# Tiles of both ends of SBUF moved to multiples of 512 bytes in a one-core S5, convolution and FFN trunk

## The chip, the core and the metric

The kernel runs on one core of a Trainium2 chip. The metric is device time in microseconds: 2323.66 us before (median of 3 runs, 2323.28 to 2326.3). The engines are named as in the profile: PE (TensorE, the matmuls), PEld (its weight loads), DVE (VectorE), ACT (ScalarE), POOL (GpSimd) and SP (SyncE, which here only starts transfers).

## The reference: what is computed

A two-layer trunk over 1024 positions of width 1024, all float32. Layer 0 mixes tokens with an S5 state-space mixer and a GLU, layer 1 with a gated width-3 convolution. Each is followed by a SwiGLU FFN (hidden 2816) and a gated per-layer input; a last RMSNorm ends it.

```python
for i in range(DEPTH):                       # DEPTH = 2
    hn = rmsnorm(h, norm_mix_g[i])
    mix = s5_mixer(hn, ...) if i % 2 == 0 else shortconv_mixer(hn, ...)
    h = h + mix
    h = h + swiglu_ffn(rmsnorm(h, norm_ffn_g[i]), ffn_w_in[i], ffn_w_out[i])
    gate = sigmoid(rmsnorm(h, norm_ple_g[i]) @ ple_w_gate[i])
    h = h + gate * (p[i] @ ple_w_up[i])
return rmsnorm(h, final_norm_g)
# s5_mixer: 64 groups of 64 complex states and 16 channels; gelu(y) @ w_glu; val * sigmoid(gate)
```

## The kernel before

**Split products.** Each float32 matrix is split into a high and a low part in the type float32r, and a product is three matmuls (`mm3`, lines 122 to 124): high by high, high by low, low by high. The first operand of `PE.matmul` after the output is the stationary one, which a weight load brings into the array (128 columns, 512 bytes per partition); the second moves through it (512 columns, 2048 bytes). In the profile's rows the moving operand is named first: `psmm<-uhigh,ws` has `uhigh` moving and `ws` stationary.

**Stages.** First the S5 stage: constants, then eight blocks of eight groups, with the two up-projections `p @ ple_w_up` (`pstu`, written out by `up<-ev`) as filler. Then GLU, FFN 0 in, FFN 0 out, the gated input of layer 0 (PLE), convolution in and out, FFN 1 in and out, PLE 1 and the final norm. The input stages (FFN in, convolution in) use `block_product`, a Strassen-like scheme of seven products of four 128-row slices with three matmuls each, 84 in all; products 0 to 3 stream `ulow`, 4 to 6 stream `uhigh`, and the weights `ws` are stationary. In the output stages the hidden tile `ch` is stationary and the weight units stream; units lie in `ulow`, `uhigh` or the four tiles `w8`. In GLU and PLE the activations in `ulow` are stationary and units in `uhigh` or `w8` stream.

**Memory.** Pools grow from both ends of SBUF. From the left: the constants (`ident`, `mhalf`, `identn`, `sgnA`, `sgnN`, `r8`, `rstd`, `cw`), then `ulow` (64 KB), then `h` and whatever the stage needs: `ws`, `st`, `hs`, `w8`, `t2` tiles. From the right: `rawp` (the four slots `raw` and `ch` and, in part, `xn`), and below it first the S5 constants (pool `s5g`, named `gen`: tables `ptab`, their scratch `ph`, `wbt`, `kp`, `dd`), later `uhigh` (48 KB). All big tiles are whole multiples of 512 bytes, so their starts modulo 512 are set by what lies at the two ends:

| tile | start before | modulo 512 | start after | modulo 512 |
|---|---|---|---|---|
| ulow | 18016 | 96 | 17408 | 0 |
| ws (lowest) | 83552 | 96 | 82944 | 0 |
| w8 (lowest, highest) | 116320, 140896 | 96 | 115712, 140288 | 0 |
| uhigh | 163808 | 480 | 163328 | 0 |
| ch, raw (lowest, highest) | 212960, 225248 | 480 | 212480, 224768 | 0 |
| t2 tiles (512 columns) | from 153440 | 352 | from 152832 | 256 |
| M, U, E, W2, tmp (S5, left) | from 120416 | 96 | from 120320 | 0 |

All slices that matmuls take of these tiles begin at multiples of 512 bytes within the tile, except in the S5 stage's own tiles.

**Order.** The order on each engine is made by a list scheduler with a simulated timeline when the kernel is built; there is no written order. It honours dependencies between tiles that share a buffer: a tile under an old tag waits until the old tile's last reader is done. DMAs are started by SP in order, the E swaps, spills and hidden stores by POOL in order.

**An S5 block b.** `gen_in` makes U and wbt, `gen_out` makes W1 and the kernel taps `kp` (16 rows), `dd` is the skip connection's diagonal, added to `kp` on POOL (line 937); `gen_toeplitz` spreads `kp` into M by eight DMAs on SP (line 950). `states` (line 963) makes pb; `scan` multiplies pb by the phases E into `tmp`, swaps its halves by two DMAs (`tw<-tmp`, line 698), adds (`sv`), scans on DVE (line 982) into `gv`, and `outputs` (lines 997 to 999) multiplies M, W1 and W2. The phase table of two blocks, `ptab`, is built on DVE by doubling in `phases`, with the scratch tile `ph`; `gen_phase` swaps it into E by four DMAs on POOL (line 957).

Of the kernel before, what the change touches and what calls it, by code (L numbers as in the profile page):

```python
# [9 lines left out]
F32 = mybir.dt.float32  # L10
F32R = mybir.dt.float32r
# [6 lines left out]

P = 128
MAGIC = 12582912.0  # L20


@with_exitstack
def trunk(
# [8 lines left out]
    V, A, G, PE = nc.vector, nc.scalar, nc.gpsimd, nc.tensor  # L33
# [8 lines left out]
    NG, NP = s5_a_re.shape[1], s5_a_re.shape[2]  # L42
    KG = D // NG
# [4 lines left out]
    const = ctx.enter_context(tc.tile_pool(name="const", bufs=1))  # L48
# [6 lines left out]
    ident = const.tile([P, P], F32, name="ident")  # L55
    make_identity(nc, ident)
    mhalf = const.tile([P, T], F32, name="mhalf")
    V.memset(mhalf, -0.5)
    identn = const.tile([P, P], F32R, name="identn")
    A.mul(identn, ident, -1.0)  # L60

# [13 lines left out]
    evp = tc.alloc_tile_pool(name="evp", bufs=2)  # L77
# [4 lines left out]
    def psum(pool=None):  # L82
        pool = pool or mm
        return pool.tile([P, 512], F32, name="ps" + pool.name, tag="ps")
# [521 lines left out]
    GB = P // KG  # L606
# [4 lines left out]
    for tl, v in ((sgnA, 1.0), (sgnN, -1.0)):  # L611
        V.memset(tl[R0], v)
        V.memset(tl[R1], -v)
    r8 = const.tile([P, NG], F32, name="r8")
    rstd = const.tile([P, T], F32, name="rstd")

    rawp = ctx.enter_context(tc.tile_pool(name="rawp", bufs=1, side="right"))
    gen = tc.alloc_tile_pool(name="s5g", bufs=1, side="right")
    st = tc.alloc_tile_pool(name="s5t", bufs=1, side="right")

    def small(shape=(P, NG), dt=F32):
        return st.tile(list(shape), dt, name="sm", tag="sm", bufs=28)

    def ts(o, a, s1, op0, s2=None, op1=None):
        if op1 is None:
            V.tensor_scalar(o, a, s1, None, op0)
        else:
            V.tensor_scalar(o, a, s1, s2, op0, op1)
        return o

    def tt(o, a, b, op):
        V.tensor_tensor(o, a, b, op)  # L632
        return o

    def stt(o, a, s, b, op0, op1):
        V.scalar_tensor_tensor(o, a, s, b, op0, op1)
        return o

    def exp_to(o, a, shape):
        n = small(shape)  # L640
        ts(n, a, 1.4426950408889634, ALU.mult, MAGIC, ALU.add)
        ts(n, n, -MAGIC, ALU.add, 129.0, ALU.min)
        ts(n, n, -127.0, ALU.max)
# [86 lines left out]
    kq = small()  # L730
    ts(kq, ang, 2.0 / math.pi, ALU.mult, MAGIC, ALU.add)
    ts(kq, kq, -MAGIC, ALU.add)
    r = small()
# [3 lines left out]
    m4 = small()  # L737
    ts(m4, kq, 0.25, ALU.mult, MAGIC, ALU.add)
    ts(m4, m4, -MAGIC, ALU.add)
    stt(m4, m4, -4.0, kq, ALU.mult, ALU.add)  # L740
# [114 lines left out]
    NJ = P // 2  # L855
    LB = 2
    LQ = LB * HQ
# [6 lines left out]
    def tmp_tile():  # L864
        return run.tile([P, GB * P], F32, name="tmp", tag="tmp", bufs=2)
# [50 lines left out]
    def gen_out(b):  # L916

        gsl = slice(b * GB, (b + 1) * GB)
        shp = [P, GB, NL, KG]
        W1 = Ws[b] = run.tile(shp, F32, name="W1", tag="W1", bufs=2)  # L920
        A.copy(W1[:, :, 0, :], cA[:, gsl])
        shp1 = [P, GB, T, KG]
        tm = tmp_tile()[:, 0:GB * P].rearrange("p (g s k) -> p g s k", g=GB, s=T)
        for o, pw, cc in ((W1[:, :, 1:NL, :], pwr, cA), (tm, pwn, cS)):
            tt(o, pw[:, gsl, 1:NL].unsqueeze(3).broadcast_to(shp1), cc[:, gsl].unsqueeze(2).broadcast_to(shp1), ALU.mult)
        tt(W1[:, :, 1:NL, :], W1[:, :, 1:NL, :], tm, ALU.subtract)
        kp = kps[b] = gen.tile([KG, GB, T, KG], F32, name="kp", tag="kp")
        for hf in range(2):
            pk = psum(tr)
            for c in range(4):  # L930
                PE.matmul(pk[0:KG, c * P:(c + 1) * P], bbA[:, b * GB + 4 * hf + c, :], W1[:, 4 * hf + c, 0:T, :],  # L931
                          start=True, stop=True)
            A.copy(kp[:, 4 * hf:4 * hf + 4].rearrange("p g s k -> p (g s k)"), pk[0:KG, :])
        dd = gen.tile([KG, GB, KG], F32, name="dd", tag="dd")
        G.tensor_tensor(dd, ident[:KG, :KG].unsqueeze(1).broadcast_to([KG, GB, KG]),
                        dk[:, gsl].unsqueeze(2).broadcast_to([KG, GB, KG]), ALU.mult)
        G.tensor_tensor(kp[:, :, 0, :], kp[:, :, 0, :], dd, ALU.add)
# [75 lines left out]
    states(0)  # L1013
    gen_phase(0)
    gen_out(0)
    gen_swap(0)
    gen_toeplitz(0, M)
    gen_in(1)
    for b in range(NBT):
        scan(b)  # L1020
        nx = b + 1
        if nx < NBT - 1:
            if b % LB == 0 and b // LB + 1 < NBT // LB:
                phases(b // LB + 1)
            gen_out(nx)
            zt = outputs(b)
            gen_phase(nx)
            states(nx)
            gen_swap(nx)
            gen_toeplitz(nx, M)  # L1030
            if b + 2 < NBT:
                gen_in(b + 2)
            channels(b, zt)
        elif nx < NBT:
            states(nx)
            gen_phase(nx)
            gen_out(nx)
            M = run.tile([P, GB, P], F32, name="M", tag="E", bufs=2)
            G.memset(M, 0.0)
            gen_toeplitz(nx, M)  # L1040
            zt = outputs(b)
            channels(b, zt)
            gen_swap(nx)
        else:
            zt = outputs(b)
# [118 lines left out]
```

## Time and profile before

| | |
|---|---|
| median of 3 runs | 2323.66 us |
| the profiled execution | 2323.06 us, of which the span is 2321.3 us |
| mean granted TensorE clock | 0.987 |
| PE, DVE, ACT, POOL busy | 96%, 57%, 33%, 7% |
| transfers waited for in the chain that ended last | DMA 3% |

The page lists groups of equal instructions by line, engine and operands: count, busy time, mean ns of one, idle time of the engine before them and what ended it. Matmuls overlap, and the end of each is modelled, so the distance from one start to the next is what tells their pace. The timeline gives a start, a duration and a merged count per row. A stretch of the view by windows gives each engine's busy time with the number of instructions.

### The profile page before, as it was taken

The page shows a single profiled execution, that of the slowest core. Times are in us where ns is not written, and L with a number is a line of the kernel's source. Part 1 is how long each engine was busy: PE and PEld are TensorE (multiplying, and loading weights), DVE is VectorE, ACT ScalarE, POOL GpSimd, SP SyncE. Part 2 cuts the span into 40 slices and gives each one's busy share as a digit, 9 for nine tenths or more (in the row PEclk, how much of TensorE's full clock was granted, in tenths as well). Part 3 has the DMA queues.
Part 4 walks back from the last instruction along what each step waited for, and adds up shares of the span by engine and source line. Part 5 has one row for each costly group of instructions (what it writes and reads, how often), then busy time and mean ns, then how long its engine had stood idle before and what let it go on. Part 6 is the DMA issues. An engine that isn't in the chain of part 4 may idle for free.

```text
span 2321.3 us, 27094 instructions
## 1 busy us (share of the span) xinstructions
PE 2240.0 (96%) x10253; PEld 1832.0 (79%) x10253; DVE 1331.0 (57%) x2244; ACT 765.3 (33%) x1449; POOL 161.8 (7%) x268
## 2 busy tenths in 40 slices
PE   6987999899999999999989999979999999999998
PEld 5776887688888888888868888868888888888887
DVE  7885325866666642224488776486666666222444
ACT  6554223433333320013343332253333333100232
POOL 2110001000000000000010000010000000000000
PEclk9999999999999999999989999989999999999999
DMA  7656201333333365433232234544333334643323
GB/s 245 149 138 150 70 19 69 103 109 109 109 109 109 109 227 181 149 119 114 89 111 84 92 94 152 192 131 118 109 109 109 109 109 141 231 163 123 127 87 109
DMA packets 212978, 288.87 MB, mean 124 GB/s; under 512 B 21360, under 2 KB 152432, under 8 KB 212848
## 3 DMA queue, kind: packets, MB, share of 16 engines
q1 hardware_dynamic: 191520, 212.63, 29.3%
q0 software_dynamic: 20928, 74.47, 10.4%
q8 instruction: 80, 1.31, 0.2%
q14 instruction: 50, 0.41, 0.1%
q10 hardware_dynamic: 400, 0.04, 0.0%
HBM read 190.93 MB, written 79.69 MB: 117 GB/s over the span
## 4 chain that ended last, share of the span: by engine, by line
PE 91%; DVE 4%; DMA 3%; ACT 1%; SPq 1%; issue 1%; POOL 0%; DVEq 0%; POOLq 0%; ACTq 0%
PE psmm L122 29%; PE psmm L124 29%; PE psmm L123 29%; PE pstr L185 1%; PE pstr L997 1%; DVE W L632 1%; DMA raw<-in_ffn_w_in_dram 1%; PE pstr L998 0%; PE pstr L999 0%; PE pstr L931 0%; DMA tw<-tmp 0%; DVE gv L982 0%; DVE tmp L632 0%; DVE xn L177 0%; PE pstu L122 0%
## 5 line engine op out<-in xcount | busy, mean ns | idle before, releaser
L122 PE MATMUL psmm<-ulow,ws 128*128 128x512 f32 x896 | 351.8, 394 | 5.7 <-ACT ws L87 3.1
L123 PE MATMUL psmm<-ulow,ws 128*128 128x512 f32 x896 | 351.5, 393 | 2.5 <-DVE ulow L88 2.5
L124 PE MATMUL psmm<-ulow,ws 128*128 128x512 f32 x896 | 351.4, 393 | 2.0 <-DVE ws L88 2.0
L124 PE MATMUL psmm<-uhigh,ws 128*128 128x512 f32 x672 | 265.3, 395 | 0.0
L122 PE MATMUL psmm<-uhigh,ws 128*128 128x512 f32 x672 | 265.0, 395 | 0.0
L123 PE MATMUL psmm<-uhigh,ws 128*128 128x512 f32 x672 | 264.9, 394 | 0.0
L409 DVE TENSOR_TENSOR h<-psmm,h 128x512 f32<-128x512 f32 x128 | 88.3, 690 | 234.4 <-PE psmm L124 234.4
L88 DVE TENSOR_TENSOR ws<-raw,ws 128x512 fp32r<-128x512 f32 x224 | 153.6, 688 | 115.1 <-ACT ws L87 115.0
L87 ACT CAST ws<-raw 128x512 fp32r<-128x512 f32 x224 | 137.8, 619 | 208.7 <-PE psmm L124 201.9
L122 PEld LDWEIGHTS psmm<-ulow,ws 128*128 128x128 f32 x896 | 169.6, 189 | 43.6 <-ACT ws L87 4.2
L123 PEld LDWEIGHTS psmm<-ulow,ws 128*128 128x128 f32 x896 | 169.6, 189 | 39.7 <-DVE ulow L88 3.5
L124 PEld LDWEIGHTS psmm<-ulow,ws 128*128 128x128 f32 x896 | 169.5, 189 | 39.1 <-DVE ws L88 3.0
L123 PE MATMUL psmm<-ulow,ch 128*128 128x512 f32 x448 | 177.2, 396 | 0.0
L122 PE MATMUL psmm<-ulow,ch 128*128 128x512 f32 x448 | 176.9, 395 | 0.0
L124 PE MATMUL psmm<-ulow,ch 128*128 128x512 f32 x448 | 176.9, 395 | 0.0
L87 ACT CAST ws<-st 128x512 fp32r<-128x512 f32 x168 | 104.2, 620 | 211.9 <-PE psmm L124 192.1
L123 PEld LDWEIGHTS psmm<-uhigh,ws 128*128 128x128 f32 x672 | 126.2, 188 | 30.3
L124 PEld LDWEIGHTS psmm<-uhigh,ws 128*128 128x128 f32 x672 | 126.1, 188 | 30.3
L122 PEld LDWEIGHTS psmm<-uhigh,ws 128*128 128x128 f32 x672 | 126.2, 188 | 29.0
L370 POOL DMA_DIRECT2D hid<-hs x104 | 78.1, 754 | 917.6 <-DVE hs L88 908.7
L140 ACT ACTIVATE junk<-h 128x512 bf16<-128x512 f32 (+1 forms) x113 | 64.1, 567 | 207.6 <-DVE h L409 122.8
L88 DVE TENSOR_TENSOR ws<-st,ws 128x512 fp32r<-128x512 f32 x168 | 115.2, 686 | 1.3 <-ACT ws L87 1.2
(241 smaller groups left out, 3997.9 us busy)
## 6 DMA issues: line engine op xcount, KB each, us to landing
hid<-hs POOLq DMA_DIRECT2D x104, 512.0 KB, 4.3
ch<-hid SPq DMA_DIRECT2D x96, 512.0 KB, 3.8
raw<-in_ffn_w_in_dram SPq DMA_DIRECT2D x88, 512.0 KB, 4.4
raw<-in_ffn_w_out_dram SPq DMA_DIRECT2D x44, 512.0 KB, 4.0
hd<-h POOLq DMA_DIRECT2D x24, 512.0 KB, 2.9
h<-hd SPq DMA_DIRECT2D x24, 512.0 KB, 5.8
raw<-in_conv_w_in_dram SPq DMA_DIRECT2D x24, 512.0 KB, 3.9
up<-ev SPq DMA_DIRECT2D x32, 256.0 KB, 3.2
```

Source lines behind the costliest of these rows:

```text
L87: A.copy(hi, src)
L88: V.tensor_tensor(lo, src, hi.bitcast(F32), ALU.subtract)
L122: PE.matmul(ps, ahi, bhi, start=start, stop=False, skip_group_check=more)
L123: PE.matmul(ps, ahi, blo, start=False, stop=False, skip_group_check=more)
L124: PE.matmul(ps, alo, bhi, start=False, stop=stop, skip_group_check=more)
L140: done["square"] = A.activation(junk[:, cs], h[t][:, cs], AF.Square, scale=1.0 / math.sqrt(D), accum_out=ms).ins
L185: PE.transpose(pt[:, c * P:(c + 1) * P], xn[:, kt * P:(kt + 1) * P], ident)
L370: nc.gpsimd.dma_start(out=hid[ht // 4][half * HT:(half + 1) * HT, :, ht % 4].rearrange("t p l j -> p t l j"), in_=hs.bitcast(F32))
L409: done["sum"] = V.tensor_tensor(h[t][:, cs], ps[nb], h[t][:, cs], ALU.add).ins
L632: V.tensor_tensor(o, a, b, op)
L997: PE.matmul(o, Us[b][:, g, :], Ms[b][:, g, :], start=True, stop=False)
```

## The change

`identn`, `r8` and `dd` leave their places: `identn` goes into the pool of evacuation tiles (left, above `h`), `r8` into `gen`, and `dd` takes part of the scratch tile `ph`. A constant `lead` of 160 bytes is added at the left, and a tile `edge` of 480 bytes, which nothing reads or writes, at the right end. The starts that follow are in the table above. `ident` stays 128 bytes over a multiple of 512.

```diff
+EDGE = 120
@@
-    identn = const.tile([P, P], F32R, name="identn")
-    A.mul(identn, ident, -1.0)
+    lead = const.tile([P, 40], F32, name="lead")
@@
-    r8 = const.tile([P, NG], F32, name="r8")
     rstd = const.tile([P, T], F32, name="rstd")
 
+    edge = ctx.enter_context(tc.tile_pool(name="edge", bufs=1, side="right"))
+    edge.tile([P, EDGE], F32, name="edge")
     rawp = ctx.enter_context(tc.tile_pool(name="rawp", bufs=1, side="right"))
     gen = tc.alloc_tile_pool(name="s5g", bufs=1, side="right")
+    r8 = gen.tile([P, NG], F32, name="r8")
+    identn = evp.tile([P, P], F32R, name="identn", bufs=1)
+    A.mul(identn, ident, -1.0)
@@
-        dd = gen.tile([KG, GB, KG], F32, name="dd", tag="dd")
+        dd = gen.tile([P, LQ * NJ], F32, name="dd", tag="ph")[0:KG, 0:P].rearrange("p (g k) -> p g k", g=GB)
         G.tensor_tensor(dd, ident[:KG, :KG].unsqueeze(1).broadcast_to([KG, GB, KG]),
                         dk[:, gsl].unsqueeze(2).broadcast_to([KG, GB, KG]), ALU.mult)
         G.tensor_tensor(kp[:, :, 0, :], kp[:, :, 0, :], dd, ALU.add)
```

The instructions are the same in number and kind. The scheduler puts some in another order, most of all in the S5 stage. On POOL, from block 0 to block 2 (`kp_1081` and `kp_1086` belong to block 1, `E_1294` and `E_1299` to block 2), before:

```order
L957 DMA E_1126<-ptab_886 64x2x256 x4
L984 MEMSET tmp_1036 128x8
L937 TENSOR_TENSOR kp_939<-kp_939,dd_952 16x8x16
L935 TENSOR_TENSOR dd_1094<-ident_72,dk_438 16x128
L937 TENSOR_TENSOR kp_1081<-kp_1081,dd_1094 16x8x16
L935 TENSOR_TENSOR dd_1262<-ident_72,dk_438 16x128
L984 MEMSET tmp_1237 128x8
L957 DMA E_1294<-ptab_1042 64x2x256 x4
L957 DMA E_1495<-ptab_1042 64x2x256 x4
L937 TENSOR_TENSOR kp_1249<-kp_1249,dd_1262 16x8x16
```

and after (lines are 4 higher there):

```order
L961 DMA E_1131<-ptab_891 64x2x256 x4
L988 MEMSET tmp_1041 128x8
L941 TENSOR_TENSOR kp_944<-kp_944,dd_957 16x8x16
L988 MEMSET tmp_1242 128x8
L939 TENSOR_TENSOR dd_1099<-ident_72,dk_443 16x128
L961 DMA E_1299<-ptab_1047 64x2x256 x4
L941 TENSOR_TENSOR kp_1086<-kp_1086,dd_1099 16x8x16
L939 TENSOR_TENSOR dd_1267<-ident_72,dk_443 16x128
L961 DMA E_1500<-ptab_1047 64x2x256 x4
L941 TENSOR_TENSOR kp_1254<-kp_1254,dd_1267 16x8x16
```

The add into block 1's `kp` stood ahead of the E swaps of block 2, which read the new table; now it stands behind them, and its `dd` waits for the table's last step. Blocks 3 and 5 are moved in the same way.

On DVE, the scan of block 3 with the end of the table for blocks 4 and 5 (`tmp` is what the tw swap sends, `sv<-sv,tw` what waits for it), before:

```order
L636 SCALAR_TENSOR_TENSOR tmp<-pb,sgnA,E 128x8x63
L632 TENSOR_TENSOR ptab<-ptab,ph 128x8x8 x2
L636 SCALAR_TENSOR_TENSOR tmp<-pb,sgnN,E 128x8x64
L632 TENSOR_TENSOR sv<-pb,E 128x8x63
L632 TENSOR_TENSOR sv<-pb,E 128x8x64
L632 TENSOR_TENSOR ph<-ptab,ew 128x256
L632 TENSOR_TENSOR ptab<-ptab,ew 128x16x16
L632 TENSOR_TENSOR ptab<-ptab,ph 128x8x16 x2
L632 TENSOR_TENSOR ph<-ptab,ew 128x512
L632 TENSOR_TENSOR ptab<-ptab,ew 128x16x32
L632 TENSOR_TENSOR sv<-sv,tw 128x8x127
L632 TENSOR_TENSOR ptab<-ptab,ph 128x8x32 x2
```

and after:

```order
L636 TENSOR_TENSOR ph<-ptab,ew 128x256
L636 TENSOR_TENSOR ptab<-ptab,ew 128x16x16
L636 TENSOR_TENSOR ptab<-ptab,ph 128x8x16 x2
L640 SCALAR_TENSOR_TENSOR tmp<-pb,sgnA,E 128x8x63
L636 TENSOR_TENSOR ph<-ptab,ew 128x512
L636 TENSOR_TENSOR ptab<-ptab,ew 128x16x32
L640 SCALAR_TENSOR_TENSOR tmp<-pb,sgnN,E 128x8x64
L636 TENSOR_TENSOR sv<-pb,E 128x8x63
L636 TENSOR_TENSOR sv<-pb,E 128x8x64
L636 TENSOR_TENSOR ptab<-ptab,ph 128x8x32 x2
L636 TENSOR_TENSOR sv<-sv,tw 128x8x127
```

The table's last two doublings, all but their final pair, stand ahead of `tmp` now, and the final pair ahead of `sv<-sv,tw`. In the GLU and all later stages the order of the products is the same up to a few places among neighbouring instructions.

## The prediction

> **What bounds the kernel now.** I read the page first: busy time, then the chain that ended last.
>
> ```profile
> span 2321.3 us, 27094 instructions
> PE 2240.0 (96%) x10253; PEld 1832.0 (79%) x10253; DVE 1331.0 (57%) x2244; ACT 765.3 (33%) x1449; POOL 161.8 (7%) x268
> PE 91%; DVE 4%; DMA 3%; ACT 1%; SPq 1%; issue 1%; POOL 0%; DVEq 0%; POOLq 0%; ACTq 0%
> ```
>
> TensorE is busy for 96% of the span and makes up 91% of the chain. That is a mean over stages, so next comes the view of busy time by stretch, one stretch for each kind of stage. Its columns are PE, PEld, DVE, ACT, POOL, granted clock, DMA share, GB/s.
>
> ```profile
> 240.00:360.00 120.00, 120.00 (x522) 97.83 (x522) 29.71 (x71) 26.68 (x77) 0.00 (x0) 1.00 0.08 26
> 480.00:820.00 340.00, 340.00 (x1482) 277.95 (x1481) 222.22 (x349) 121.65 (x211) 26.95 (x36) 1.00 0.38 112
> 1250.00:1440.00 190.00, 190.00 (x829) 155.25 (x828) 138.50 (x204) 62.04 (x95) 13.16 (x25) 1.00 0.33 106
> 0.00:220.00 220.00, 178.53 (x1171) 149.92 (x1171) 167.64 (x429) 121.82 (x291) 36.33 (x71) 0.95 0.65 169
> ```
>
> In the GLU (240 to 360 us), the first FFN (480 to 820) and the convolution's input products (1250 to 1440) TensorE never pauses, at granted clock 1.00, and the next busiest engine, VectorE, has 27% of its time left even in the tightest (138.50 of 190). There only the step from one matmul to the next sets the time. The S5 stage (0 to 220) is different: TensorE 178.53 of 220 us, VectorE 167.64, DMA share 0.65; they wait for one another in turn.
>
> So the question is what a matmul's step depends on. The timeline of TensorE answers it, if one takes the first and last row of stretches in which one kind of matmul runs without a break. The operand named first streams ("moving"), the second is loaded as weights ("stationary"); `w` is the tile w8.
>
> ```profile
> 266.54 0.39 PE L122 MATMUL psmm<-w,ulow 128*128 128x512 f32 x1
> ...
> 309.86 0.39 PE L124 MATMUL psmm<-w,ulow 128*128 128x512 f32 x1
> 310.08 0.40 PE L122 MATMUL psmm<-uhigh,ulow 128*128 128x512 f32 x1
> ...
> 354.65 0.39 PE L124 MATMUL psmm<-uhigh,ulow 128*128 128x512 f32 x1
> 499.44 0.39 PE L123 MATMUL psmm<-ulow,ws 128*128 128x512 f32 x1
> ...
> 507.17 0.39 PE L124 MATMUL psmm<-ulow,ws 128*128 128x512 f32 x1
> 507.39 0.40 PE L122 MATMUL psmm<-uhigh,ws 128*128 128x512 f32 x1
> ...
> 512.75 0.39 PE L124 MATMUL psmm<-uhigh,ws 128*128 128x512 f32 x1
> 843.77 0.40 PE L122 MATMUL psmm<-ulow,ch 128*128 128x512 f32 x1
> ...
> 933.14 0.39 PE L124 MATMUL psmm<-ulow,ch 128*128 128x512 f32 x1
> 933.37 0.39 PE L122 MATMUL psmm<-uhigh,ch 128*128 128x512 f32 x1
> ...
> 944.34 0.39 PE L122 MATMUL psmm<-uhigh,ch 128*128 128x512 f32 x1
> ```
>
> The duration column (0.39 or 0.40) is modelled and tells nothing; the steps do. `w,ulow`: 192 matmuls (8 row tiles of 8 x 3), 43.32 us over 191 steps, 226.8 ns. `uhigh,ulow`: 192, 44.57 us over 191, 233.4 ns. `ulow,ws`: 35 in 7.73 us, 227.4 ns. `uhigh,ws`: 24 in 5.36 us, 233.0 ns. `ulow,ch`: 384 (8 row tiles, 2 halves, 8 hidden tiles x 3), 89.37 us over 383 steps, 233.3 ns. From 933.37 to 944.34 stand one row tile's 48 matmuls, 36 `uhigh,ch` and 12 `w,ch`; with the 12 at 233.3, the 36 take (10.97 - 2.80)/36 = 226.9 ns.
>
> Neither operand explains this alone: `ulow` moves at 227.4 with `ws` and at 233.3 with `ch`; `uhigh` moves at 233.0 with `ws` and at 226.9 with `ch`. The pair does. `ulow`, `ws` and `w8` are tiles of the left end (96 over a multiple of 512 bytes), `uhigh` and `ch` of the right end (480 over). **Both operands from one end: 227.0 ns. One from each end: 233.2 ns.** The two left starts in `w,ulow` are up to 120 KB apart and the step is still the short one, so distance as such is not it. Within one end all slices differ by multiples of 512 bytes; across the ends the difference is 384 over such a multiple.
>
> **The change, part by part.** First, all large tiles of both ends now start at multiples of 512 bytes, so every pair stands as pairs within one end do today. How many matmuls have one operand from each end is in the groups by line; L123 and L124 have equal counts, so each row stands for three.
>
> ```profile
> L122 PE MATMUL psmm<-uhigh,ws 128*128 128x512 f32 x672 | 265.0, 395 | 0.0
> L122 PE MATMUL psmm<-ulow,ch 128*128 128x512 f32 x448 | 176.9, 395 | 0.0
> L122 PE MATMUL psmm<-uhigh,ulow 128*128 128x512 f32 x256 | 100.9, 397 | 0.6 <-ACT uhigh L87 0.6
> L122 PE MATMUL psmm<-w,ch 128*128 128x512 f32 x192 | 76.2, 397 | 0.0
> L122 PE MATMUL psmm<-ulow,ws 128*128 128x512 f32 x896 | 351.8, 394 | 5.7 <-ACT ws L87 3.1 <-ACT ulow L87 1.9 <-ACT s L348 0.7
> L122 PE MATMUL psmm<-w,ulow 128*128 128x512 f32 x248 | 96.9, 391 | 0.0
> L122 PE MATMUL psmm<-uhigh,ch 128*128 128x512 f32 x192 | 74.8, 390 | 0.0
> ```
>
> Mixed pairs: 3 x (672 + 448 + 256 + 192) = 4704. One-end pairs: 3 x (896 + 248 + 192) = 4008. At 233.2 - 227.0 = 6.2 ns, little of it behind waits (idle before the mixed groups is 0.0 to 0.6 us), the first term is 4704 x 6.2 ns = **-29 us**. Bounds: 0, if the ends and not the offsets matter; and -29 - 111 = -140, if landing on a 512 multiple also removes what a one-end pair still pays (third rival). I take -29, since both offsets that the trace shows (96 with 96, 480 with 480) give the same 227 ns: the difference between the two counts, not the offset itself.
>
> A rule of the Trainium skill speaks against this term. "SBUF — State Buffer" (Who interferes with whom) gives TensorE two read ports, one for the moving operand and one for the weight load, and calls them independent. By that rule the weights' place could not matter to the step and the term would be 0 (the first rival); the 233.3 beside 226.9 ns for the same `ch` disagrees with it.
>
> Second, the diagonal term `dd` now lives in the phase table's scratch tile `ph`, and the scheduler has moved work in the S5 stage. GpSimd must wait to write `dd` until VectorE has finished the current table, and four E swaps now stand between `dd` and the add into `kp`. `kp` feeds the eight M transfers on SP, and M the outputs' first matmul (L997). Rows of the timeline for block 1 (73.84 to 95.76) and block 3 (120.11 to 137.98), and the landing row of tile M:
>
> ```profile
> 73.84 1.02 POOL L937 TENSOR_TENSOR kp<-kp,dd 16x128 f32<-16x128 f32 x1 [14.96 <-DMA up<-ev]
> 87.94 0.73 DVE L632 TENSOR_TENSOR ptab<-ptab,ph 128x256 f32<-128x256 f32 x2
> 88.97 2.41 POOL L957 DMA_DIRECT2D E<-ptab  x4 [8.42 <-DVE ptab L632]
> 85.80 3.84 SPq L950 DMA_DIRECT2D M<-kp  x6
> 95.76 0.49 PE L997 MATMUL pstr<-M,U 128*128 128x128 f32 x2
> 120.11 0.41 DVE L632 TENSOR_TENSOR ph<-ptab,ew 128x256 f32<-128x256 f32 x1
> ...
> 122.03 0.68 DVE L632 TENSOR_TENSOR ptab<-ptab,ew 128x512 f32<-128x512 f32 x1
> 124.71 0.75 DVE L632 TENSOR_TENSOR ptab<-ptab,ph 128x256 f32<-128x256 f32 x2
> 137.98 0.49 PE L997 MATMUL pstr<-M,U 128*128 128x128 f32 x2
> DMA to landing us min/median/max: 1.9/2.7/7.1
> ```
>
> Block 1: the table ends at 88.67; `dd` (0.4, estimated from the add's kind), four E swaps 2.41 and an add of at most 1.02 bring `kp` to 92 instead of 74.9; eight M issues at 0.64 (3.84/6) end at 97, and 1.9 to 2.7 to land makes 99 to 99.8 against an L997 at 95.76: 3 to 4 us late. Queued behind L997 on TensorE are the other output products and the next block's transposes, behind M on SP the tw transfers of block 2. Half of it, +2, I let reach the end, since VectorE waits for tw there anyway. Block 3: the table ends at 125.46 and L997 stands at 137.98; 0.4 + 2.41 + 1.02 + 5.1 + 2.7 = 11.6 us still fit between. But five table steps, 2.6 us (120.11 to 122.71), now stand ahead of the `tmp` that releases tw, where before they filled the wait for tw; in exchange the last pair (0.75) moves ahead of `sv`: +1.9. Block 5 has two such steps of the 0.41 kind: +0.8. Together +4.7, and as a few short steps also move into block 2's wait, I take **+4 us**, with bounds -2 (the trade only swaps idle time) and +8 (all of 4 + 2.6 + 0.8 reaches the end).
>
> Third, `identn` (into the evacuation pool) and `r8` (into the S5 pool) are the same instructions at other addresses. VectorE's and ScalarE's operands already come from both ends: priced 0. DMA: VectorE waits for tw for 23.7 us in the S5 stage, eight times; were aligned rows 10% quicker, 2 us would go, so 0 with a bound of -2.
>
> ```profile
> DVE sv L632 <- DMA tw<-tmp: 23.7, 8, 5.5
> ```
>
> The profiled execution took 2323.06 us (span 2321.3 and 1.8 around it), 0.6 under the median of the runs. 2323.1 - 29 + 4 = 2298, as a median 2298.7.
>
> **The rivals.** *The ends decide, not the offsets* (13%): something between the two regions, such as memory split into parts, lengthens mixed pairs wherever they start. `uhigh` begins some 15 KB above the highest `w8`, and a border there would look the same in this trace; against it, operands in separate parts should disturb each other less. Then only S5 moves: 2323.1 + 4 + 0.6 = 2328.
>
> *Half of it* (8%): the mixed steps alternate or keep part of their price, say 3 ns: -15 + 4, 2313.
>
> *Multiples of 512 remove more* (5%). What a one-end pair pays beyond streaming can be read where the last tile's matmuls are 256 wide:
>
> ```profile
> 2307.76 0.28 PE L122 MATMUL psmm<-w,ulow 128*128 128x256 f32 x1
> ...
> 2309.44 0.28 PE L124 MATMUL psmm<-w,ulow 128*128 128x256 f32 x1
> ```
>
> 14 steps in 1.68 us, 120.0 ns, against 226.8 for 512: 0.417 ns a column, so 12.8 ns a matmul are fixed. If that is a cost of starting 32 bytes off and goes, 8712 x 12.8 = 111 us more: 2187. Against it: 96 and 480 pay alike. "TensorE: Matmul & The Clock Gate" of the Trainium skill (Wait — 56ns, not 53.3ns?) has 215.7 ns back to back at 512 columns, which would be 11 ns under the trace's best; no run here shows it.
>
> *Slower: equal offsets collide* (5%). At a multiple of 512 both streams of every pair open the same line or bank, and the 6.2 ns falls on the 4008 one-end pairs too, while the mixed keep theirs: +25 + 4, 2352. It decides from the first GLU matmul on (266 us). Against it, equal offsets are today's quick case.
>
> **How the numbers follow.** Alike offsets 69%, own range 2291 to 2304 (S5 -2 to +8, step 5.7 to 6.5 ns). Range 2290 to 2328: it takes in the half case and the first rival. A change under 0.2% (4.6 us) is about what a measurement of this kernel cannot tell from none. Faster: 69 + 8 + 5 and a lucky 1 of the first rival, 83%. The first rival's 2328 lies just within 0.2%: 8% same, and 4% with the 5% of the collision slower, 9%.
>
> **What would show it.** Right: `uhigh,ws`, `ulow,ch`, `uhigh,ulow` and `w,ch` step at 227 like `ulow,ws`; a row tile of `uhigh,ch` and `w,ch` takes 10.90 us, not 10.97; FFN tiles come every 84 x 227 = 19.07 us, not 19.29; GLU starts 2 to 8 us later than 221.7 and everything after it has gained 29. Wrong: mixed steps still at 233 (first rival), steps near 214 (third), one-end steps at 233 (fourth), or L997 of blocks 3 and 5 waiting for M.

## The result and the profile after

The changed kernel takes **2296.8 us** (median of 4 runs, 2293.95 to 2299.36) against 2324.06 us of the kernel before in the same session (4 runs, 2323.28 to 2326.3): a ratio of **0.9881**, 95% interval 0.9864 to 0.9898, or 27 us less. Two later sessions gave 0.9887 and 0.9882. The profiled execution took 2295.76 us.

The page of the changed kernel, its span, busy times and chain:

```profile
span 2293.8 us, 27089 instructions
PE 2214.1 (97%) x10253; PEld 1832.5 (80%) x10253; DVE 1332.0 (58%) x2244; ACT 768.2 (33%) x1449; POOL 167.3 (7%) x268
PE 89%; DVE 3%; DMA 1%; ACT 1%; issue 0%; POOL 0%; DVEq 0%; SPq 0%; ACTq 0%; POOLq 0%
```

The same 10253 matmuls, PE busy for 26 us less, and still the bound. The view by stretches (PE, PEld, DVE, ACT, POOL, granted clock, DMA share, GB/s) shows the same work done denser, not less idle: PE was full in these stretches before and is full now, and has started more matmuls in each (531, 1501 and 839; before 522, 1482 and 829).

```profile
240.00:360.00 120.00, 120.00 (x531) 99.38 (x530) 30.30 (x73) 27.07 (x78) 0.00 (x0) 1.00 0.09 26
480.00:820.00 340.00, 340.00 (x1501) 281.53 (x1500) 220.44 (x347) 124.61 (x213) 27.02 (x36) 1.00 0.34 110
1250.00:1440.00 190.00, 190.00 (x839) 157.19 (x838) 136.62 (x201) 61.05 (x93) 15.22 (x28) 1.00 0.37 124
```

The timeline of TensorE in the changed kernel, first and last rows of the stretches that the prediction read:

```profile
310.00 0.39 PE L122 MATMUL psmm<-uhigh,ulow 128*128 128x512 f32 x1
...
353.29 0.39 PE L124 MATMUL psmm<-uhigh,ulow 128*128 128x512 f32 x1
503.81 0.39 PE L122 MATMUL psmm<-uhigh,ws 128*128 128x512 f32 x1
...
509.02 0.39 PE L124 MATMUL psmm<-uhigh,ws 128*128 128x512 f32 x1
836.10 0.47 PE L122 MATMUL psmm<-ulow,ch 128*128 128x512 f32 x1 [0.29 <-DMA ch<-hid]
...
923.26 0.39 PE L122 MATMUL psmm<-uhigh,ch 128*128 128x512 f32 x1
...
934.14 0.39 PE L122 MATMUL psmm<-uhigh,ch 128*128 128x512 f32 x1
```

`uhigh,ulow`: 43.29 us over 191 steps, 226.6 ns (before 233.4). `uhigh,ws`: 5.21 us over 23, 226.5 (233.0). `ulow,ch`: from 836.10 to the first matmul behind the 384 of them, 87.16 us over 384 steps, 227.0 with the slower first step (233.3). One row tile of 48 `uhigh,ch` and `w,ch`: 10.88 us (10.97). One FFN tile of 84, from the start of a `ulow,ws` at 495.88 to that at the same place of the next tile, 514.92: 19.04 us. No mixed pair is left that is slower than the others.

Where the 27 us went, by the starts of the stages' first matmuls in the two profiled executions:

| from one first matmul to the next | before, us | after, us | difference |
|---|---|---|---|
| start to GLU (S5) | 221.71 | 222.70 | +1.0 |
| GLU and FFN 0's entry | 188.10 | 185.69 | -2.4 |
| FFN 0 in | 433.96 | 427.71 | -6.3 |
| FFN 0 out | 248.69 | 243.86 | -4.8 |
| PLE 0 | 105.81 | 104.75 | -1.1 |
| convolution in | 242.86 | 242.75 | -0.1 |
| convolution out | 106.04 | 102.73 | -3.3 |
| FFN 1 in | 426.50 | 421.93 | -4.6 |
| FFN 1 out | 248.64 | 243.86 | -4.8 |
| PLE 1 to the last matmul | 91.09 | 90.06 | -1.0 |

Two rows don't fit a mere change of pace. The convolution's input stage has gained nothing, though its 432 mixed matmuls also step at 226.7, which by itself is a gain of 2.8 us; FFN 0 in has gained 1.7 more than FFN 1 in. The waits of TensorE in the convolution's input stage tell why, first of the kernel before, then of the changed one (waited for, us in total, times, longest; two more waits are the same in both):

```profile
PE psmm L122 <- ACT ws L87: 1.9, 2, 1.3
```

```profile
PE psmm L122 <- ACT ulow L87: 2.7, 1, 2.7
PE psmm L122 <- ACT ws L87: 1.3, 1, 1.3
```

A wait of 2.7 us for ScalarE's cast of `ulow` is new at the stage's entry. The scheduler has not only moved S5 work: it also ordered the casts at the entries of the input stages anew. At FFN 0's entry the same kind of wait was there in the kernel before, and is gone after:

```profile
PE psmm L122 <- ACT ulow L87: 1.9, 1, 1.9
```

### The profile page after: what moved, and what is told of

It reads as the page before. It is cut to its first block, busy times and chain, and to the rows that moved or that the text cites. A ratio compares the mean times of both kernels' runs of the same rounds, so it can differ in the third digit from the quotient of the medians.

```text
span 2293.8 us, 27089 instructions
## 1 busy us (share of the span) xinstructions
PE 2214.1 (97%) x10253; PEld 1832.5 (80%) x10253; DVE 1332.0 (58%) x2244; ACT 768.2 (33%) x1449; POOL 167.3 (7%) x268
## 3 DMA queue, kind: packets, MB, share of 16 engines
q0 software_dynamic: 20928, 74.47, 9.1%
## 4 chain that ended last, share of the span: by engine, by line
PE 89%; DVE 3%; DMA 1%; ACT 1%; issue 0%; POOL 0%; DVEq 0%; SPq 0%; ACTq 0%; POOLq 0%
PE psmm L124 28%; PE psmm L123 28%; PE psmm L122 28%; PE pstr L185 1%; DVE xn L177 0%; PE pstr L935 0%; DVE gv L986 0%; PE pstr L1001 0%; PE pstr L1003 0%; DVE ulow L88 0%; DMA raw<-in_ffn_w_in_dram 0%; DVE W L636 0%; PE pstr L1002 0%; DMA ch<-hid 0%; DVE tmp L636 0%
## 5 line engine op out<-in xcount | busy, mean ns | idle before, releaser
L122 PE MATMUL psmm<-uhigh,ws 128*128 128x512 f32 x672 | 261.4, 389 | 0.0
L123 PE MATMUL psmm<-uhigh,ws 128*128 128x512 f32 x672 | 261.4, 389 | 0.0
L124 PE MATMUL psmm<-uhigh,ws 128*128 128x512 f32 x672 | 261.2, 389 | 0.0
L122 PE MATMUL psmm<-ulow,ch 128*128 128x512 f32 x448 | 174.5, 390 | 0.3 <-DMA ch<-hid 0.3
L123 PE MATMUL psmm<-ulow,ch 128*128 128x512 f32 x448 | 174.6, 390 | 0.0
L124 PE MATMUL psmm<-ulow,ch 128*128 128x512 f32 x448 | 174.3, 389 | 0.0
```

Source lines behind the costliest of these rows:

```text
L122: PE.matmul(ps, ahi, bhi, start=start, stop=False, skip_group_check=more)
L123: PE.matmul(ps, ahi, blo, start=False, stop=False, skip_group_check=more)
L124: PE.matmul(ps, alo, bhi, start=False, stop=stop, skip_group_check=more)
```

## Experiments

Each run is given with its ratio to the kernel before on the same chip. D is short for the distance between the starts of the two ends, modulo 512 bytes.

| kernel | left, right start mod 512 | order | time, us | ratio, 95% interval |
|---|---|---|---|---|
| before | 96, 480 | before | 2323.2 to 2324.1 | 1 |
| changed | 0, 0 | changed | 2296.8; again 2296.3, 2296.6 | 0.9881; 0.9887, 0.9882 |
| offsets undone | 96, 480 | changed | 2328.6 | 1.0024, 1.0015 to 1.0033 |
| both at 480 | 480, 480 | changed | 2300.5; again 2299.6 | 0.9902; 0.9900 |
| both at 480, `dd` apart | 480, 480 | before | 2293.8; again 2291.7 | 0.9872; 0.9860 |
| right at 256 | 0, 256 | changed | 2296.4 | 0.9880, 0.9864 to 0.9897 |
| half `dd` apart, right at 256 | 0, 256 | before on PE and ACT | **2289.5** | **0.9855**, 0.9838 to 0.9871 |

### Only the offsets undone

```diff
-    lead = const.tile([P, 40], F32, name="lead")
+    lead = const.tile([P, 64], F32, name="lead")
-    edge = ctx.enter_context(tc.tile_pool(name="edge", bufs=1, side="right"))
-    edge.tile([P, EDGE], F32, name="edge")
```

> The changed kernel, instruction for instruction, with the offsets of the kernel before: left end 96, right end 480 over a multiple of 512 (padding 256 bytes, nothing free at the right end). Only the S5 order of the change is left. Theory D: mixed pairs at 233.2, one-end pairs at 227.1 ns, as before the change. For the S5 term: if the new order costs 4 us by itself (the prediction) and the new places gave 3 of them back, the GLU's first matmul stands at 225 to 226 us and the time at 2327 to 2328; if the order costs only the 1 us that the trace after shows, GLU at 222.4 to 223 and the time at 2324 to 2325.

2328.6 us, ratio 1.0024 (1.0015 to 1.0033): **5.3 us slower than before**. The timeline of TensorE has the mixed step back, 44.56 us over 191 steps, 233.3 ns:

```profile
311.63 0.40 PE L122 MATMUL psmm<-uhigh,ulow 128*128 128x512 f32 x1
...
356.19 0.39 PE L124 MATMUL psmm<-uhigh,ulow 128*128 128x512 f32 x1
```

So the 233 ns come from the offsets and nothing else in the change. The S5 expectation missed with both its branches: the GLU's first matmul stands at 223.10 us, next to the second branch, but the time is next to that of the first. The rest is behind S5: the convolution's input stage takes 247.13 us instead of 242.86 (a wait of 3.4 us for the cast of `ulow` at its entry), FFN 0 in 1.1 less. From GLU's first matmul to the last one it is 2094.74 us against 2091.69 before: the new order costs 3 us there.

### Both ends at 480

```diff
-    lead = const.tile([P, 40], F32, name="lead")
+    lead = const.tile([P, 32], F32, name="lead")
-    edge = ctx.enter_context(tc.tile_pool(name="edge", bufs=1, side="right"))
-    edge.tile([P, EDGE], F32, name="edge")
```

> The changed kernel, instruction for instruction, with the constants' padding 128 bytes instead of 160 and nothing left free at the right end: the tiles of both ends start 480 bytes over a multiple of 512. Theory D (the difference of the two operands' starts, modulo 512, sets the step): every pair steps at 226.7 to 227.1 ns, 2295 to 2299 us, as the changed kernel within 0.1%. Theory M (a start on the multiple of 512 itself is what quickens): what was mixed stays near 233, or all pairs rise together, 2310 to 2326 us. Between them: the one-end pairs at 227.1 as before the change and not at 226.7 would put 8712 x 0.4 ns = 3.5 us on the multiple itself.

2300.5 us, 0.9902 (0.9889 to 0.9916), 1.5 us above the time expected. The timeline of TensorE: 43.29 us over 191 steps, 226.6 ns.

```profile
313.94 0.39 PE L122 MATMUL psmm<-uhigh,ulow 128*128 128x512 f32 x1
...
357.23 0.39 PE L124 MATMUL psmm<-uhigh,ulow 128*128 128x512 f32 x1
```

Theory D holds: a start 480 bytes over the multiple is as quick as one on it, when both operands have it. The one-end pairs, too, step at 226.7 (mean over the 2637 `ulow,ws` steps without a wait; 227.4 before), so their small excess does not hang on the multiple. It went with the mixed pairs beside them: in the kernel before, 321 of the 353 `ulow,ws` steps above 230 ns are among the first three behind a mixed matmul, and from the fourth on they step at 226.7. Yet the time is 3.7 us above the changed kernel, and GLU starts at 226.66 us. That was tried again side by side:

> The changed kernel again, beside the kernel with both ends at 480 on one chip. If a start on the multiple of 512 itself is worth something outside the pairs (transfers, VectorE, ScalarE), this one stays some 3.7 us below it, as in their separate runs (2296.8 and 2300.5); if the 3.7 us are a difference of runs, the two agree within 1.5 us.

> The kernel with both ends 480 over a multiple of 512 again, all else as the changed kernel, beside the changed kernel: 2299 to 2302 us if the multiple itself counts, within 1.5 us of the changed kernel if not.

2296.3 us (2295.7 to 2302.1) and 2299.6 us (2297.5 to 2305.5). The medians stand 3.3 us apart as in the first pair, but the ranges overlap: likely, not settled.

### The order of before kept, both ends at 480

```diff
-        dd = gen.tile([P, LQ * NJ], F32, name="dd", tag="ph")[0:KG, 0:P].rearrange("p (g k) -> p g k", g=GB)
+        dd = gen.tile([KG, GB, KG], F32, name="dd", tag="dd")
```

with the padding of 128 bytes and nothing free at the right end, as above; the 512 bytes that the offsets no longer need hold `dd`.

> As the first of these runs (both ends 480 over a multiple of 512), with dd in a tile of its own of 512 bytes, for which there is room again: every engine has the order of the kernel before. Theory D: 226.7 to 227.1 ns for all pairs. S5: if the new places quicken the stage by 3 us and the order costs 4, GLU starts at 218.5 to 219.5 and the time is 2292 to 2294; if the order costs 1 us and the places nothing, GLU starts at 221.5 to 222 and the time is 2294.5 to 2297, below the changed kernel by 1 us.

2293.8 us (2291.5 to 2296.7) against 2300.5 (2299.6 to 2303.8) of the same offsets with the changed order: the order costs **6.7 us**. The time is that of the first S5 branch, but GLU starts at 222.12 us, as in the second: the profiled execution, 2295.72 us, is one of the two longer ones of four, so the S5 expectation is not settled by it. With the old order the convolution's input stage takes 239.77 us, 3.1 less than before, which is the gain that the changed kernel lacked there. Again beside the changed kernel:

> Both ends at 480 with dd in a tile of its own, again, beside the changed kernel: 2293 to 2295 us, 2 to 3 us under the changed kernel, if its order is what it gains; equal to the changed kernel within 1 us if the first run was lucky.

> The changed kernel once more, as the measure for the other two: 2296 to 2297 us.

2291.7 us (2289.8 to 2292.8) and 2296.6 us (2295.7 to 2297.7): the ranges don't touch, and the 5.0 us between them are more than the 2 to 3 expected.

### Is it 512? The pairs alone

A kernel of stretches of 48 matmuls each; it leaves out all of the reference's computation. During a stretch nothing else is at work but one copy of the last result on VectorE, 0.69 us of some 11.

```python
def stretch(name, m, s, n=48, a=None, b=None, w=512):
    a, b = a or mv, b or st                             # moving and stationary tile
    t = ps.tile([P, 512], F32, name=name, tag="t")
    for i in range(n):
        mo, so = m + 512 * (i % 7), s + 128 * (i % 16)  # float32 columns
        PE.matmul(t[:, 0:w], b[:, so:so + 128], a[:, mo:mo + w], start=i == 0, stop=i == n - 1)
    V.tensor_copy(res[:, 0:w], t[:, 0:w])
```

> Leaves all of the reference's work out: only stretches of 48 matmuls of 128x128 by 128x512 in one block each, on copies of the input, with no other engine at work during a stretch. Moving tile at a multiple of 512 and weights 0, 32, 64 ... 480 bytes over one (st0 to st480); weights at 0 and moving 4 to 480 over (mv4 to mv480); both over by the same (both4 to both480); and widths 256 and 384. Theory D: st0 and all both-stretches 226.7 to 227.1, st128 and st384 and mv384 about 233, and the row of st shows which differences cost. If the 6 ns is TensorE against the other engines' traffic in one part of the memory (a rival that the traces leave open), all stretches step at 227. If the absolute start counts, both4, both32 and both96 lie above both of st0.

Worked out from the starts of the matmuls within each stretch, without its first step, moving tile at a multiple of 512:

| weights over it by, bytes | 0 | 32 | 64 | 96 | 128 | 160 | 192 | 224 |
|---|---|---|---|---|---|---|---|---|
| step, ns | 226.7 | 233.3 | 233.3 | 234.3 | 232.5 | 233.3 | 228.9 | 233.3 |
| the same plus 256, ns | 226.7 | 233.3 | 233.3 | 234.3 | 232.5 | 233.3 | 228.9 | 233.3 |

**The period is 256 bytes, not 512.** The other way round, weights at the multiple and moving tile 96, 256, 384 or 480 over it, the steps are 233.4, 227.5, 233.2 and 233.3. With the other engines idle the loss is nearly as large as in the kernel (5.8 to 6.5 ns at 384 bytes, 6.5 there), so it is TensorE's own doing: moving stream against weights. Both operands over by the same 32, 96, 256 or 480: 226.9, 227.5, 227.5, 227.1; both 4 over: 239.1. Distance 0 is quick at the multiples of 32 tried, but not at 4.

### Right end at 256 in the whole kernel

```diff
-EDGE = 120
+EDGE = 56
```

> The changed kernel with the right end 256 bytes over a multiple of 512 (224 bytes left free instead of 480); the left stays on the multiple. The stretches alone gave 226.7 ns for weights 256 over and 232.5 for 128 and 384 over, so the period would be 256 and not 512: then all pairs step at 226.7 here too, and the time is that of the changed kernel within 1.5 us. If the kernel's pairs need the full 512 (the prediction's reading), the 4704 mixed ones are back at 232 to 233: 2322 to 2327 us.

2296.4 us, 0.9880 (0.9864 to 0.9897), the changed kernel's time. The timeline of TensorE, 384 matmuls of `ulow,ch` and the first behind them, 87.16 us, 227.0 ns as in the changed kernel:

```profile
837.78 0.47 PE L122 MATMUL psmm<-ulow,ch 128*128 128x512 f32 x1 [0.71 <-DMA ch<-hid]
...
924.94 0.39 PE L122 MATMUL psmm<-uhigh,ch 128*128 128x512 f32 x1
```

224 bytes left free do what 480 do.

### Which weights meet which stream

> Leaves all of the reference's work out: stretches of 48 matmuls as before. In 'inphase' moving tile and weights both alternate between 0 and 128 bytes over a multiple of 512, so that each matmul's own two operands agree, but the weights of the next differ by 128 from what streams; in 'crossed' each matmul's own operands differ by 128, and the weights of the next agree with what streams. If the weights being loaded for the next matmul meet the stream of the present one, inphase steps at 232 to 233 ns and crossed at 226.7; if a matmul's own pair counts, inphase 226.7 and crossed 232 to 233. Widths 128 to 448, on the multiple and 128 over: if what is lost is a fixed time per weight load, about the same 5.8 ns at every width whose step leaves the load no idle time, and less at narrow ones.

The timeline of TensorE in that kernel; a row is one stretch, and the start of the next row less its own, over 48, is its step. Names give the bytes by which the weights (w), or both, lie over the multiple of 512, or the width (n).

```profile
31.12 11.04 PE L49 MATMUL zero<-mv,st 128*128 128x512 f32 x48
42.00 11.36 PE L49 MATMUL w64over<-mv,st 128*128 128x512 f32 x48
...
97.41 11.13 PE L49 MATMUL inphase<-mv,st 128*128 128x512 f32 x48
108.38 11.20 PE L49 MATMUL crossed<-mv,st 128*128 128x512 f32 x48
119.42 11.64 PE L49 MATMUL both4over<-mv,st 128*128 128x512 f32 x48
...
241.32 7.20 PE L49 MATMUL n320zero<-mv,st 128*128 128x320 f32 x48
248.36 7.20 PE L49 MATMUL n320over<-mv,st 128*128 128x320 f32 x48
255.40 8.51 PE L49 MATMUL n384zero<-mv,st 128*128 128x384 f32 x48
263.75 8.61 PE L49 MATMUL n384over<-mv,st 128*128 128x384 f32 x48
272.19 9.89 PE L49 MATMUL n448zero<-mv,st 128*128 128x448 f32 x48
281.92 9.95 PE L49 MATMUL n448over<-mv,st 128*128 128x448 f32 x48
291.70 11.04 PE L49 MATMUL last<-mv,st 128*128 128x512 f32 x48
```

`zero` 10.88/48 = 226.7; from rows not shown, `w64over` 233.1, `w128over` 232.5, `w192over` 229.2, `w256over` 227.3, `w384over` 232.3: the table above again. `inphase` 228.5 and `crossed` 230.0: both expectations fail. Neither the own pair alone nor the next matmul's weights alone sets the step; each arrangement pays a part. Nor is it a fixed time per weight load: 128 over costs nothing at 320 columns (146.7 ns each), 1.9 ns at 384 (8.35 against 8.44 us), 1.0 at 448 (9.73 against 9.78), 5.8 at 512. What in TensorE's reads collides stays open. What the runs show is that at starts on multiples of 32 the distance modulo 256 sets the step to within about a nanosecond.

### A version with both

Left end at 0, right end at 256, and `dd` in 256 bytes of its own, four groups at a time:

```diff
-EDGE = 120
+EDGE = 56
-        dd = gen.tile([P, LQ * NJ], F32, name="dd", tag="ph")[0:KG, 0:P].rearrange("p (g k) -> p g k", g=GB)
-        G.tensor_tensor(dd, ...)
-        G.tensor_tensor(kp[:, :, 0, :], kp[:, :, 0, :], dd, ALU.add)
+        for hf in range(2):
+            hs_, hg = slice(4 * hf, 4 * hf + 4), slice(b * GB + 4 * hf, b * GB + 4 * hf + 4)
+            dd = gen.tile([KG, GB // 2, KG], F32, name="dd", tag="dd")
+            G.tensor_tensor(dd, ..., dk[:, hg]..., ALU.mult)
+            G.tensor_tensor(kp[:, hs_, 0, :], kp[:, hs_, 0, :], dd, ALU.add)
```

> A version meant to keep both halves of what the runs so far showed: left end on the multiple of 512, right end 256 over (224 bytes left free), and dd in a tile of its own again, 256 bytes for four of a block's eight groups at a time, so that TensorE and ScalarE have the order of the kernel before; GpSimd does two small pairs per block instead of one. If the order of the change costs what the pair of runs at 480 says (about 6 us) and the left end at 480 costs some 3 us in the S5 stage, this one comes to 2290 to 2292 us; if only the order counts, to 2293 to 2295, as the kernel with both ends at 480 and dd apart; if four more small GpSimd steps per two blocks delay M, to 2296 or more.

**2289.5 us** (2288.9 to 2292.1), 0.9855 (0.9838 to 0.9871): 34 us below the kernel before and 7.1 below the changed one of the same session, whose range it doesn't touch, and half a microsecond below its first branch. Its range does overlap that of the kernel with both ends at 480 and `dd` apart, 2289.8 to 2292.8 in the same session, so what the left end adds is not settled by it. GLU starts at 218.94 us; TensorE still waits for M, by `PE pstr L1002 <- DMA M<-kp: 2.9, 2, 2.7` in its list of waits up to there.

## Why the prediction came out right

2298.0 was forecast as an execution and 2298.7 as a median; 2296.8 was measured. The likeliest case was the one that happened, but part of the agreement is luck: errors that cancel.

**Step 1, mixed pairs step like one-end pairs: right.** -29 us was the term. From GLU's first matmul to the last one the trace went from 2091.69 us (before) or 2094.74 (before's offsets, changed order) to 2063.35 us: with the order held fixed, **-31.4 us**; and 2091.69 to 2060.96 in the half-`dd` version, -30.7. The term was a little short: all pairs now step at 226.7, so 4704 of them gained 233.2 - 226.7 = 6.5 ns, -30.6, and the one-end pairs lost their small excess over it.

The reason given, "the difference between the two counts, not the offset itself", holds by the run with both ends at 480. "Multiples of 512" was too narrow: the trace of before held only the differences 0 and 384, and could not tell 512 from 256.

The rule of the Trainium skill that was weighed against it, independent read ports for the moving operand and the weight load ("SBUF — State Buffer", Who interferes with whom), doesn't describe this: with nothing else at work but one short VectorE copy per stretch, weights 128 bytes off cost 5.8 ns a matmul.

**Step 2, the S5 order, +4 us: near in size, wrong in one of its costs and in part of its path.** Block 1's first output matmul comes 6.8 us later (102.53 against 95.76), not 3 to 4. Rows of the changed kernel's timeline, on GpSimd, SP, TensorE and VectorE:

```profile
87.68 4.71 POOL L939 TENSOR_TENSOR dd<-ident,dk 16x128 f32<-16x128 f32 x1 [8.20 <-DVE ptab L636]
92.34 2.42 POOL L961 DMA_DIRECT2D E<-ptab  x4
94.73 0.45 POOL L941 TENSOR_TENSOR kp<-kp,dd 16x128 f32<-16x128 f32 x1
95.26 0.40 POOL L939 TENSOR_TENSOR dd<-ident,dk 16x128 f32<-16x128 f32 x1
95.21 5.21 SPq L954 DMA_DIRECT2D M<-kp  x8
102.53 0.77 PE L1001 MATMUL pstr<-M,U 128*128 128x128 f32 x2 [6.27 <-DMA M<-kp]
87.45 1.22 DVE L636 TENSOR_TENSOR raw<-pwr,bbA 128x1024 f32<-128x1024 f32 x1
88.59 1.22 DVE L636 TENSOR_TENSOR raw<-pwn,bbS 128x1024 f32<-128x1024 f32 x1
89.72 1.21 DVE L636 TENSOR_TENSOR W<-W,tmp 128x1024 f32<-128x1024 f32 x1
90.86 1.28 DVE L636 TENSOR_TENSOR tmp<-gv,E 128x504 f32<-128x504 f32 x2
96.83 0.74 DVE L640 SCALAR_TENSOR_TENSOR tmp<-pb,sgnA,E 128x504 f32<-128x504 f32 x1 [3.23 <-DMA E<-ptab]
```

The chain is the one that the prediction laid out (`dd`, four E swaps, the add, eight M transfers, landing), and the swaps, the add and the issues took what was priced. The mis-sized term is `dd`: **4.71 us instead of 0.4**. It ran beside five VectorE instructions that each read two SBUF operands; the next one, at 95.26, with VectorE idle, took 0.40. That is what the Trainium skill states in "SBUF — State Buffer" (Who interferes with whom): a VectorE instruction with two SBUF inputs contends with a GpSimd instruction that reads SBUF. The trace agrees with 4.71 against 0.40 us, and GpSimd stayed shut out over several such instructions in a row; the longest `dd` took 4.71 or 4.72 us in all seven profiles with the changed order.

The E swaps stand behind `dd` too, at 92.34 instead of 88.97, and that is a path that the prediction did not have: the scan of block 2 (`tmp`, 96.83) waits 3.23 us for them. The row of the kernel before waits 0.71:

```profile
95.31 0.74 DVE L636 SCALAR_TENSOR_TENSOR tmp<-pb,sgnA,E 128x504 f32<-128x504 f32 x1 [0.71 <-DMA E<-ptab]
```

What it made of the scans is best read at equal offsets, the kernel before against the run with the offsets undone, by the start of each block's `sv<-sv,tw` on VectorE:

| block | 1 | 2 | 3 | 5 | 7 |
|---|---|---|---|---|---|
| before, us | 80.40 | 102.74 | 123.58 | 164.12 | 201.71 |
| offsets undone, us | 79.59 | 106.07 | 128.49 | 169.24 | 206.75 |
| later by | -0.8 | 3.3 | 4.9 | 5.1 | 5.0 |

So 4.1 us arose up to block 2, where +2 was priced, 1.6 in block 3 (+1.9) and 0.2 behind it (+0.8 in block 5).

What of it reached the GLU, by the starts of its first matmul:

| GLU's first matmul, us | order of before | changed order |
|---|---|---|
| left end on a multiple of 512 | 218.94 | 222.70, 222.17, 223.05, 224.07 |
| left end at 96 or 480 | 221.71, 222.12, 220.86 | 223.10, 226.66, 224.86 |

By the means the order costs 223.0 - 218.9 = 4.1 us in the upper row and 224.9 - 221.6 = 3.3 in the lower. Single executions of one kernel differ by up to 2 us here, and the upper left has but one. Pair by pair the cost is 4.5 and 4.0 us with both ends at 480 but 1.4 at the offsets of before (223.10 - 221.71). The odd one out is the kernel before: its last block has a wait of TensorE of a length that no other of these executions has there (2.9 us at most), which fits:

```profile
PE pstr L997 <- DMA W<-W: 6.5, 1, 6.5
```

So the S5 term lies between 1.4 and 4.5 us, and +4 is in its upper part. Blocks 3 and 5 did not wait for M: TensorE's waits for M in the changed kernel are 6.3 us in block 1 and 0.5 us in block 7, the last.

**Step 3, places and DMA at 0 with a bound of -2: not refuted, not settled.** The sign "GLU starts 2 to 8 us later" failed: it starts 1.0 us later. The rows of the table differ by 2.6 us (order of before) and 1.9 us (changed order) in favour of a left end on the multiple, but the run at 96 with the changed order, 223.10, lies among the four above it. What the offsets do change are the transfers. The row of SP's queue from 0 to 220 us, of the kernel before and of the changed one (packets, MB, share of 16 engines):

```profile
q1 hardware_dynamic: 30176, 32.25, 55.2%
```

```profile
q1 hardware_dynamic: 30176, 32.25, 49.9%
```

The same packets and bytes take a tenth less time. All five profiles with the left end on a multiple of 512 show 49.5% to 50.2% there, all six with it at 96 or 480 53.6% to 55.4%. This is the "aligned rows 10% quicker" that the prediction named without counting on it. But VectorE's wait for tw, from which it took its 2 us, is 20.8 us with the offsets undone and 20.6 in the changed kernel. That the quicker transfers bring GLU forward is not shown.

**What the prediction did not have:** the order also moved casts at the entries of FFN 0 and of the convolution, a wait of 1.9 us gone in one and one of 2.7 us come in the other. The part on the change says that later stages keep their order up to a few places; in the traces ScalarE's order differs at the entries of all three input stages. At the old offsets it costs 2094.74 - 2091.69 = 3.0 us. At alike ones the means from GLU to the end are 2063.7 (six executions with the changed order) and 2061.9 us (three with the order of before), 1.8 apart, but one of the three, 2064.0, lies inside the range of the six.

So -25 was forecast as -29 + 4, all of the 4 in S5. The run with the offsets undone splits the 27.4 us between the two profiled executions: +1.4 (order, in S5) + 3.0 (order, behind S5) - 0.4 (offsets, in S5) - 31.4 (offsets, behind S5). The order's whole cost, 4.4 us here and 5.3 by the medians of that run and the kernel before, is near the +4 only because a part that nobody priced made up for what S5 did not show, and its excess made up for part of the 2.4 us that the pairs gave beyond -29.

One sum is off: the fixed part of a one-end matmul is 2 x 120.0 - 226.8 = 13.2 ns, not 12.8, which makes the third rival's bound 115 us instead of 111. The forecast does not rest on it.

**The rivals.** *The ends decide* falls: pairs from two ends are quick at alike offsets. *Half of it* falls: 226.7 throughout. *Multiples of 512 remove more* falls: the step is 226.6 ns with both starts on a multiple, as with both 480 over one. *Equal offsets collide* falls: equal is the quick case.

## What to carry to other kernels

Before tuning what TensorE does, look whether matmuls of one shape have two paces in the trace, and compare where their two operands start: here, with 512 columns, moving and stationary tiles whose starts differ by a multiple of 256 bytes stepped at 226.7 ns, all other distances in steps of 32 at 229 to 234. The cheapest padding that makes the distance right is enough for the matmuls, and what it takes the room from must not be a buffer that orders the work. A list scheduler's new order has to be priced at every stage that it touches, and a GpSimd instruction that reads SBUF beside a run of VectorE work on two SBUF operands at the length of that run: here 4.71 us instead of 0.40.

## What the hardware showed that was not expected

- The loss depends on the distance modulo 256 and not evenly: 192 costs 2.2 ns, 128 costs 5.8, the others 6.6 to 7.6.
- It depends on the width: at the same distance of 128, nothing at 320 columns, 1.9 ns at 384, 1.0 at 448, 5.8 at 512.
- Both operands 4 bytes over a multiple of 512, at distance 0, step at 239 ns, slower than any distance at multiples of 32.
- A small GpSimd product on 16 partitions took 4.71 us beside five VectorE instructions and 0.40 without.
- SP's queue took 49.9% of the transfer engines' time in the first 220 us with the left end on a multiple of 512 bytes, 55.2% with it at 96, for the same 30176 packets.
- GpSimd's queue took 9.1% of the transfer engines' time for its 74.47 MB over the whole span with the left end at a multiple of 512, 10.4% to 10.7% with it at 96 or 480.
